# Seven half-size products in the first matmul as well, with part of the sums as accumulating transfers

## The chip, the cores and the metric

One core of one Trainium2 chip. The metric is device time in microseconds (us), the median over the runs of a kernel. The profile's span is shorter than the time (about 1.8 us for the kernel before); the text says which of the two a number is. A run counts as slow when it lies over 1.5% above the fastest run of the same kernel; ratios use fast runs only.

## The reference

```python
m, k, n, p = 1024, 1024, 2048, 1024
h = np.matmul(a, b)                                     # 1024 x 2048
h = 0.5 * h * (1 + np.tanh(np.sqrt(2 / np.pi) * (h + 0.044715 * h ** 3)))
return np.matmul(h, c).astype(np.float32)               # 1024 x 1024
```

## The kernel before

The first product is plain: 16 column tiles of b times two halves of 512 rows of a, 8 matmuls each, in bf16. The second is done with seven products of half-size quarters instead of eight, Winograd's form of Strassen's scheme: it needs sums of quarters of h (s1 to s4) and of c (t1 to t4), and VectorE makes all of them. The sums are fp32r (4 bytes), the plain quarters bf16 (2 bytes) where they are used only as they are.

```python
    # first product: six tiles while b arrives, then the rest
    for k in range(KT):
        ...
        for t in range(N0):
            nc.tensor.matmul(ps[t], bt(k, t), aT[0][:, k, :],
                             start=(k == 0), stop=(k == KT - 1))
    # ... cut ...
    def mm1(t, h):
        p = ppool.tile([128, H], F32, name="ps")
        for k in range(KT):
            nc.tensor.matmul(p, bt(k, t), aT[h][:, k, :],
                             start=(k == 0), stop=(k == KT - 1))
        gelu(t, h, p)
    # ... cut ...
    def sum_s4(i):
        nc.vector.tensor_tensor(pair(s2, i), h12[:, ts(i, 2), :], pair(s2, i), op=SUB)

    def sum_t4(t):
        nc.vector.tensor_tensor(t2[t], t2[t], c21[:, t:t + 1, :], op=SUB)
    # ... cut ...
    for j in R:                                  # s3 x t3, beside it s4 on VectorE
        p = bank()
        prod(p, whole(s3), whole(t3), j)
        nc.vector.tensor_tensor(u3[:, j, :], p, u2[j], op=ADD)
        sum_s4(j)
    for j in R:                                  # s1 x t1 (p5), beside it t4 on VectorE
        p = bank()
        prod(p, whole(s1), pairs(t1), j)
        combine(4 + j, 1, p, u3[:, j, :])
        nc.vector.tensor_tensor(u2[j], p, u2[j], op=ADD)
        sum_t4(2 * j)
        sum_t4(2 * j + 1)
    # ... cut: s4 x c22, h22 x t4, the last tile ...
```

Of the kernel before, what the change touches and what calls it, by code (L numbers as in the profile page):

```python
# [19 lines left out]
def kernel(ctx, tc, a, b, c, out):  # L20
# [22 lines left out]
    b0stage = ctx.enter_context(tc.tile_pool(name="b0stage", bufs=8))  # L43
# [9 lines left out]
    NH = NT // 2  # L53
    aT = [keep.tile([128, KT, H], BF16, name=f"aT{h}", tag=f"A{h}") for h in range(2)]
    WB = W0 + W1
    b_lo = keep.tile([128, KT, WB], BF16, name="b_lo", tag="B0")
    b_hi = keep.tile([128, KT, N - WB], BF16, name="b_hi", tag="B1")

    def bcols(k0, kn, n0, w):
        if n0 < WB:  # L60
            return b_lo[:, k0:k0 + kn, ds(n0, w)]
        return b_hi[:, k0:k0 + kn, ds(n0 - WB, w)]

    def bt(k, t):
        return bcols(k, 1, t * 128, 128)[:, 0, :]


    hq = [[keep.tile([128, NH, H], F32R if h else BF16, name=f"h{h}{g}") for g in range(2)]
          for h in range(2)]
# [19 lines left out]
    for mt in range(4):  # L89
        load_a0(mt, 2 if mt == 3 else 1)  # L90
# [38 lines left out]
    for mt in range(4):  # L129
        if mt < 3:  # L130
            ab.append(cast_a0(mt + 1))
        turn0(mt, ab[mt], (0,) if mt == 3 else (0, 1))
        if mt < 3:
            warm_up(3)
    cast_b0(0)
    for k in range(KT):
        if k + 1 < KT:
            cast_b0(k + 1)
        for t in range(N0):
            nc.tensor.matmul(ps[t], bt(k, t), aT[0][:, k, :],  # L140
                             start=(k == 0), stop=(k == KT - 1))
        if k == 0:
            turn0(3, ab[3], (1,))

    def gelu(t, h, p):
        nc.scalar.activation(hq[h][t // NH][:, t % NH, :], p, AF.Gelu_apprx_tanh)  # L146

    for t in range(N0):
        gelu(t, 0, ps[t])


    def load_b(k0, kn, n0, w):
        nc.gpsimd.dma_start(out=bcols(k0, kn, n0, w), in_=bv[:, k0:k0 + kn, ds(n0, w)])

    ps = [(tpool if t < 2 else ppool).tile([128, H], F32, name="pt" if t < 2 else "ps")
          for t in range(N1)]
    for k in range(0, KT, 4):
        load_b(k, 4, W0, W1)
        for i in range(4):
            for t in range(N1):  # L160
                nc.tensor.matmul(ps[t], bt(k + i, N0 + t), aT[0][:, k + i, :],  # L161
                                 start=(k + i == 0), stop=(k + i == KT - 1))
    for t in range(N1):
        gelu(N0 + t, 0, ps[t])


    def mm1(t, h):
        p = ppool.tile([128, H], F32, name="ps")
        for k in range(KT):
            nc.tensor.matmul(p, bt(k, t), aT[h][:, k, :],  # L170
                             start=(k == 0), stop=(k == KT - 1))
        gelu(t, h, p)

    W2 = 384
    for n0 in range(W0 + W1, N, W2):
        for k in range(0, KT, 4):
            load_b(k, 4, n0, W2)

    a1 = []
    for j in range(4):  # L180
        st = abf.tile([128, K], BF16, name="ab1")
        nc.gpsimd.dma_start(out=st, in_=av[:, 4 + j, :])
        a1.append(st)

    def turn(j):
        ab = a1[j]
        pt = tpool.tile([128, KT, 128], BF16, name="pt")
        for k in range(KT):
            nc.tensor.transpose(pt[:, k, :], ab[:, ts(k, 128)], ident)  # L189
        nc.vector.tensor_copy(aT[1][:, :, ts(j, 128)], pt)  # L190

    for t in range(N0 + N1, NT):
        mm1(t, 0)
        if t == NT - 3:
            turn(0)
        if t == NT - 2:
            turn(1)
            turn(2)
            turn(3)
# [7 lines left out]
    (h11, h12), (h21, h22) = hq  # L207
    c11 = keep.tile([128, NH, H], BF16, name="c11")
    c21 = keep.tile([128, NH, H], BF16, name="c21")
    c22 = keep.tile([128, NH, H], F32R, name="c22")  # L210
    c12 = keep.tile([128, NH, H], BF16, name="c12", tag="A0")
# [5 lines left out]
    load_c(c11, 0, 0)  # L217
    load_c(c22, 1, 1)
    load_c(c21, 1, 0)
    load_c(c12, 0, 1)  # L220

    t1 = [astage.tile([128, 2, H], F32R, name="t1", tag="a_st") for _ in range(4)]
    t2 = [b0stage.tile([128, 1, H], F32R, name="t2", tag="b0_st") for _ in range(8)]
    s1 = keep.tile([128, NH, H], F32R, name="s1")

    def sum_t1(i):
        nc.vector.tensor_tensor(t1[i], c12[:, ts(i, 2), :], c11[:, ts(i, 2), :], op=SUB)  # L227

    def sum_t2(t):
        nc.vector.tensor_tensor(t2[t], c22[:, t:t + 1, :], t1[t // 2][:, t % 2:t % 2 + 1, :], op=SUB)  # L230

    def sum_s1(t):
        nc.vector.tensor_tensor(s1[:, t, :], h21[:, t, :], h22[:, t, :], op=ADD)

    for t in range(NT):
        mm1(t, 1)
        if 3 <= t < 7:
            sum_t1(t - 3)
        if 6 <= t < 10:
            sum_t2(2 * (t - 6))  # L240
            sum_t2(2 * (t - 6) + 1)
        if t == WB // 128:
            t3 = keep.tile([128, NH, H], F32R, name="t3", tag="B0")
        if t >= NH + 1:
            sum_s1(t - NH - 1)
        if WB // 128 <= t < WB // 128 + 4:
            i = t - WB // 128
            nc.vector.tensor_tensor(t3[:, ts(i, 2), :], c22[:, ts(i, 2), :], c12[:, ts(i, 2), :], op=SUB)
    sum_s1(NH - 1)

    s2 = [keep.tile([128, NH // 2, H], F32R, name=f"s2{g}", tag=f"A{g}") for g in range(2)]

# [12 lines left out]
    def sum_t4(t):
        nc.vector.tensor_tensor(t2[t], t2[t], c21[:, t:t + 1, :], op=SUB)

    def bank(w=H):
        return ppool.tile([128, w], F32, name="ps", padded_shape=[128, H])

    def prod(p, lhs, rhs, j, q=slice(0, H)):
        for t in range(NH):
            nc.tensor.matmul(p, lhs(t)[:, ts(j, 128)], rhs(t)[:, q],  # L273
                             start=(t == 0), stop=(t == NH - 1))
# [98 lines left out]
```

## Time and profile before

| | before |
|---|---|
| time, median (3 runs) | 123.95 us |
| span of the profiled run | 122.1 us |
| TensorE busy | 116.1 us (95%) |
| VectorE busy | 64.6 us (53%) |
| first product ends, second begins | 69.0 us |
| second product, up to TensorE's end | 50.2 us |

The page divides the span into 40 slices; a digit is the busy share in tenths. The chain of waits is followed back from the last instruction: what stands in it sets the end, what does not could be longer without harm. For TensorE the starts of successive matmuls give the real pitch, because the listed durations overlap. The prediction shows these lines.

### The profile page before, as it was taken

The numbers are of one execution on the slowest core, as the hardware profiler recorded it, in microseconds if no ns is written. First come the engines' busy times: TensorE is split into PE (matmuls) and PEld (weight loads), VectorE is DVE, ScalarE is ACT, GpSimd is POOL, SyncE is SP. The second block draws the span as 40 slices with busy tenths as digits, with TensorE's granted clock in tenths as the row PEclk, the third lists the DMA queues.
The fourth block names the chain that finished last, engine by engine and source line by source line (L and its number), as shares of the span: only waits on it lengthen the run. The fifth ranks groups of instructions, "written<-read, shape, count | busy, mean of one in ns | idle before, by whom it ended". The sixth has DMA issues, their size and how long they took to land.

```text
span 122.1 us, 1486 instructions
## 1 busy us (share of the span) xinstructions
PE 116.1 (95%) x577; PEld 68.3 (56%) x577; DVE 64.6 (53%) x95; ACT 30.7 (25%) x54; POOL 21.5 (18%) x26
## 2 busy tenths in 40 slices
PE   6977999999998999999999999999999999999990
PEld 2542444444456444444444444468888888888880
DVE  0352340000014200006999999999769999974351
ACT  4454752806331133233323331100000000000000
POOL 2000099132440220000000000797000000000000
PEclk9999999999999999999999999999999999999999
DMA  3999969999999999995000000000600022445425
GB/s 144 351 328 347 413 188 191 198 200 205 209 207 206 329 394 231 206 206 97 0 0 0 5 0 3 3 0 0 258 0 0 5 86 86 157 167 191 163 99 167
DMA packets 12582, 18.44 MB, mean 151 GB/s; under 512 B 800, under 2 KB 7584, under 8 KB 12576
## 3 DMA queue, kind: packets, MB, share of 16 engines
q0 software_dynamic: 7968, 8.91, 39.6%
q1 hardware_dynamic: 4464, 9.37, 20.9%
q10 hardware_dynamic: 144, 0.07, 0.2%
q8 instruction: 4, 0.07, 0.2%
q14 instruction: 2, 0.02, 0.0%
HBM read 20.97 MB, written 4.19 MB: 206 GB/s over the span
## 4 chain that ended last, share of the span: by engine, by line
PE 88%; DMA 6%; SPq 2%; DVE 1%; ACT 0%; issue 0%
PE ps L273 41%; PE ps L170 31%; PE ps L140 8%; DMA b_st<-in_b_dram 6%; PE ps L161 3%; PE pt L161 3%; SPq L78 2%; PE pt L189 1%; DVE aT L190 1%; ACT b_lo L126 0%; SPq L85 0%; DVE ot L342 0%; PE pt L115 0%
## 5 line engine op out<-in xcount | busy, mean ns | idle before, releaser
L146 ACT ACTIVATE h<-ps 128x512 fp32r<-128x512 f32 (+1 forms) x30 | 17.3, 602 | 28.6 <-PE ps L170 26.3
L170 PE MATMUL ps<-aT,b_hi 128*128 128x512 bf16 x96 | 21.4, 379 | 0.0
L170 PE MATMUL ps<-aT,b_lo 128*128 128x512 bf16 x80 | 17.4, 379 | 0.0
L170 PEld LDWEIGHTS <-b_hi 128*128 128x128 bf16 x96 | 9.3, 98 | 10.8
L273 PE MATMUL ps<-t,s 128*128 128x512 f32 x64 | 15.0, 392 | 0.0
L273 PE MATMUL ps<-t,h 128*128 128x512 f32 x64 | 14.8, 389 | 0.0
L273 PE MATMUL ps<-c,h 128*128 128x512 bf16 (+2 forms) x80 | 14.2, 336 | 0.0
L313 POOL COPY lk<-u 128x512 f32<-128x512 f32 x1 | 7.7, 7684 | 33.6 <-ACT u L306 33.6
L273 PEld LDWEIGHTS ps<-t,s 128*128 128x128 f32 x64 | 12.0, 188 | 2.6
L273 PEld LDWEIGHTS ps<-t,h 128*128 128x128 f32 x64 | 12.0, 188 | 2.5
L170 PEld LDWEIGHTS <-b_lo 128*128 128x128 bf16 x80 | 7.8, 98 | 9.4
L227 DVE TENSOR_TENSOR t<-c,c 128x1024 fp32r<-128x1024 bf16 x4 | 4.7, 1222 | 15.8 <-DMA c<-in_c_dram 15.7
L190 DVE COPY aT<-pt 128x1024 bf16<-128x1024 bf16 x4 | 2.7, 689 | 19.4 <-PE pt L189 19.3
L140 PE MATMUL ps<-aT,b_lo 128*128 128x512 bf16 x48 | 10.9, 380 | 0.8 <-DVE b_lo L125 0.8
L273 PEld LDWEIGHTS <-h 128*128 128x128 bf16 x80 | 7.2, 98 | 7.0 <-issue 0.3
L140 PEld LDWEIGHTS <-b_lo 128*128 128x128 bf16 x48 | 4.5, 98 | 6.6 <-DVE b_lo L125 1.1
L215 POOL DMA_DIRECT2D c<-in_c_dram x8 | 5.9, 744 | 11.7 <-PE ps L170 6.0
L296 DVE TENSOR_TENSOR ot<-ps,u 128x512 f32<-128x512 f32 x11 | 7.3, 684 | 1.1 <-PE ps L273 1.1
L101 PE MATMUL ps<-warm 128*128 128x512 bf16 x17 | 6.3, 516 | 1.2 <-DVE warm L49 1.2
L273 PE MATMUL ps<-c,s 128*128 128x512 f32 x32 | 7.4, 389 | 0.0
L273 PEld LDWEIGHTS ps<-c,s 128*128 128x128 f32 x32 | 6.0, 188 | 1.2
L125 DVE CAST b_lo<-b_st 128x384 bf16<-128x384 f32 x8 | 2.9, 368 | 5.1 <-DMA b_st<-in_b_dram 5.1
(40 smaller groups left out, 96.5 us busy)
## 6 DMA issues: line engine op xcount, KB each, us to landing
out_dram<-ot SPq DMA_DIRECT2D x15, 256.0 KB, 2.0
c<-in_c_dram POOLq DMA_DIRECT2D x6, 512.0 KB, 14.8
b_st<-in_b_dram SPq DMA_DIRECT2D x7, 384.0 KB, 8.1
c<-in_c_dram POOLq DMA_DIRECT2D x2, 1024.0 KB, 15.0
a_st<-in_a_dram SPq DMA_DIRECT2D x3, 512.0 KB, 4.1
b_hi<-in_b_dram POOLq DMA_DIRECT2D x4, 384.0 KB, 11.3
b_lo<-in_b_dram POOLq DMA_DIRECT2D x2, 512.0 KB, 7.2
ab<-in_a_dram POOLq DMA_DIRECT2D x4, 256.0 KB, 13.9
```

Of the source, the lines that this page charges most:

```text
L101: nc.tensor.matmul(ps[N0 - 1], warm[:, 0:128], warm, start=True, stop=True)
L125: nc.vector.tensor_copy(b_lo[:, k, 0:HW], b_st[k][:, 0:HW])
L140: nc.tensor.matmul(ps[t], bt(k, t), aT[0][:, k, :], start=(k == 0), stop=(k == KT - 1))
L146: nc.scalar.activation(hq[h][t // NH][:, t % NH, :], p, AF.Gelu_apprx_tanh)
L161: nc.tensor.matmul(ps[t], bt(k + i, N0 + t), aT[0][:, k + i, :], start=(k + i == 0), stop=(k + i == KT - 1))
L170: nc.tensor.matmul(p, bt(k, t), aT[h][:, k, :], start=(k == 0), stop=(k == KT - 1))
L190: nc.vector.tensor_copy(aT[1][:, :, ts(j, 128)], pt)
L215: nc.gpsimd.dma_start(out=dst[:, t:t + 4, :], in_=cv[:, r * NH + t:r * NH + t + 4, ts(q, H)])
L227: nc.vector.tensor_tensor(t1[i], c12[:, ts(i, 2), :], c11[:, ts(i, 2), :], op=SUB)
L273: nc.tensor.matmul(p, lhs(t)[:, ts(j, 128)], rhs(t)[:, q], start=(t == 0), stop=(t == NH - 1))
L296: nc.vector.tensor_tensor(ot, u if swap else p, p if swap else u, op=op)
L313: nc.gpsimd.tensor_copy(last_keep, last)
```

## The change

The intent is to take 16 of the 256 matmuls of the first product away as well. The right half of b (1024 columns) is treated as four quarters; with the four quarters of a it gives h12 and h22 from seven products of 16 matmuls. The left half stays plain. That needs six new sums before these products and two between them. To make room on VectorE, several sums become accumulating transfers: ScalarE or an earlier sum fills the destination, and a transfer issued by GpSimd adds the second operand into it. Three such groups come late: t3, s2 + h12 (s4) and t2 + c21 (t4). The product s1 × t1 (p5) goes second in the last block, and half-width matmuls fill the time between the last turns (transposes) of a. The first stage loads 1024 columns of b instead of 768.

```diff
-    W0 = N0 * 128
+    W0 = N // 2
...
+    for i in range(2):                       # six new sums, two tiles each
+        tt(as1[i], aT[1][:, P2[i], :], aT[1][:, P2[i + 2], :], op=ADD)
+    # ... as2, as3, bt3, b12, bt2 cut ...
+    for j in R:
+        p = bank()
+        prod(p, KH, pairs(bt2), pairs(as2), j)
+        tt(v2[:, j, :], p, v2[:, j, :], op=ADD)
+    for i in range(2):
+        nc.gpsimd.dma_start(out=as2[i], in_=aT[0][:, P2[i + 2], :], accum_op=ADD)
+    for i in range(2):
+        nc.gpsimd.dma_start(out=bt2[i], in_=bx[:, P2[i + 2], :], accum_op=ADD)
+    # ... four more of the seven products cut ...
+    for i in R:                              # t2 = t1 - c22
+        nc.scalar.mul(t2[i], c22[:, P2[i], :], -1.0)
+        nc.gpsimd.dma_start(out=t2[i], in_=t1[:, P2[i], :], accum_op=ADD)
+    c21 = keep.tile([128, NH, H], BF16, name="c21", tag="BX")
+    load_c(c21, 1, 0)
...
     for j in R:
         p = bank()
-        prod(p, whole(h11), whole(c11), j)
-        nc.scalar.activation(u2[j], p, AF.Copy)
+        prod(p, NH, whole(h11), whole(c11), j)
+        nc.scalar.activation(p1[:, j, :], p, AF.Copy)
+    for i in (2, 3, 0, 1):                   # t3 = c22 - c12
+        nc.scalar.mul(t3p(i), c12[:, P2[i], :], -1.0)
+        nc.gpsimd.dma_start(out=t3p(i), in_=c22[:, P2[i], :], accum_op=ADD)
+    # ... p5 = s1 x t1, s3, then u2 = s2 x t2 cut ...
+    for g in range(2):                       # s4 = s2 + h12
+        nc.gpsimd.dma_start(out=s2[g], in_=h12[:, ts(g, KH), :], accum_op=ADD)
+    for i in R:                              # t4 = t2 + c21
+        nc.gpsimd.dma_start(out=t2[i], in_=c21[:, P2[i], :], accum_op=ADD)
+    # ... h12 x c21, s3 x t3, s4 x c22, h22 x t4, the last tile cut ...
```

More of the change, by code (lines that the diff above doesn't have):

```diff
@@ L29 @@
     N0 = 6
-    W0 = N0 * 128
-    N1 = 4
-    W1 = N1 * 128
+    W0 = N // 2
+    KH = KT // 2
+    NH = NT // 2
+    R = range(4)
     av = a.rearrange("(mt p) k -> p mt k", p=128)
@@ L42 @@
     abf = ctx.enter_context(tc.tile_pool(name="abf", bufs=4))
-    b0stage = ctx.enter_context(tc.tile_pool(name="b0stage", bufs=8))
+    b0stage = ctx.enter_context(tc.tile_pool(name="b0stage", bufs=6))
     opool = ctx.enter_context(tc.tile_pool(name="opool", bufs=4))
@@ L51 @@
     make_identity(nc, ident)
-    NH = NT // 2
     aT = [keep.tile([128, KT, H], BF16, name=f"aT{h}", tag=f"A{h}") for h in range(2)]
-    WB = W0 + W1
-    b_lo = keep.tile([128, KT, WB], BF16, name="b_lo", tag="B0")
-    b_hi = keep.tile([128, KT, N - WB], BF16, name="b_hi", tag="B1")
-    def bcols(k0, kn, n0, w):
-        if n0 < WB:
-            return b_lo[:, k0:k0 + kn, ds(n0, w)]
-        return b_hi[:, k0:k0 + kn, ds(n0 - WB, w)]
-    def bt(k, t):
-        return bcols(k, 1, t * 128, 128)[:, 0, :]
-    hq = [[keep.tile([128, NH, H], F32R if h else BF16, name=f"h{h}{g}") for g in range(2)]
-          for h in range(2)]
+    a22 = keep.tile([128, KH, H], F32R, name="a22", tag="A22")
+    b_lo = keep.tile([128, KT, W0], BF16, name="b_lo", tag="B0")
+    bx = keep.tile([128, KT, H], BF16, name="bx", tag="BX")
+    b12 = keep.tile([128, KH, H], F32R, name="b12", tag="BT")
+    b22 = keep.tile([128, KH, H], F32R, name="b22", tag="BR")
+    (h11, h12), (h21, h22) = [[keep.tile([128, NH, H], F32R if h else BF16, name=f"h{h}{g}")
+                               for g in range(2)] for h in range(2)]
     a_st, b_st = {}, {}
@@ L88 @@
     gate = consts.tile([128, 1], F32, name="gate")
-    for mt in range(4):
+    for mt in R:
         load_a0(mt, 2 if mt == 3 else 1)
@@ L128 @@
     ab = [cast_a0(0)]
-    for mt in range(4):
+    for mt in R:
         if mt < 3:
@@ L139 @@
         for t in range(N0):
-            nc.tensor.matmul(ps[t], bt(k, t), aT[0][:, k, :],
+            nc.tensor.matmul(ps[t], b_lo[:, k, ts(t, 128)], aT[0][:, k, :],
                              start=(k == 0), stop=(k == KT - 1))
@@ L143, with gelu, bank @@
             turn0(3, ab[3], (1,))
-    def gelu(t, h, p):
-        nc.scalar.activation(hq[h][t // NH][:, t % NH, :], p, AF.Gelu_apprx_tanh)
+    def gelu(dst, src):
+        nc.scalar.activation(dst, src, AF.Gelu_apprx_tanh)
+    def bank(w=H):
+        return ppool.tile([128, w], F32, name="ps", padded_shape=[128, H])
     for t in range(N0):
-        gelu(t, 0, ps[t])
-    def load_b(k0, kn, n0, w):
-        nc.gpsimd.dma_start(out=bcols(k0, kn, n0, w), in_=bv[:, k0:k0 + kn, ds(n0, w)])
-    ps = [(tpool if t < 2 else ppool).tile([128, H], F32, name="pt" if t < 2 else "ps")
-          for t in range(N1)]
-    for k in range(0, KT, 4):
-        load_b(k, 4, W0, W1)
-        for i in range(4):
-            for t in range(N1):
-                nc.tensor.matmul(ps[t], bt(k + i, N0 + t), aT[0][:, k + i, :],
-                                 start=(k + i == 0), stop=(k + i == KT - 1))
-    for t in range(N1):
-        gelu(N0 + t, 0, ps[t])
-    def mm1(t, h):
-        p = ppool.tile([128, H], F32, name="ps")
-        for k in range(KT):
-            nc.tensor.matmul(p, bt(k, t), aT[h][:, k, :],
-                             start=(k == 0), stop=(k == KT - 1))
-        gelu(t, h, p)
-    W2 = 384
-    for n0 in range(W0 + W1, N, W2):
-        for k in range(0, KT, 4):
-            load_b(k, 4, n0, W2)
+        gelu(h11[:, t, :], ps[t])
     a1 = []
-    for j in range(4):
+    for j in R:
         st = abf.tile([128, K], BF16, name="ab1")
@@ L183 @@
         a1.append(st)
+    nc.gpsimd.dma_start(out=b12, in_=bv[:, 0:KH, W0 + H:N])
+    nc.gpsimd.dma_start(out=b22, in_=bv[:, KH:KT, W0 + H:N])
+    for k in range(0, KT, KH):
+        nc.gpsimd.dma_start(out=bx[:, k:k + KH, :], in_=bv[:, k:k + KH, W0:W0 + H])
     def turn(j):
-        ab = a1[j]
         pt = tpool.tile([128, KT, 128], BF16, name="pt")
         for k in range(KT):
-            nc.tensor.transpose(pt[:, k, :], ab[:, ts(k, 128)], ident)
+            nc.tensor.transpose(pt[:, k, :], a1[j][:, ts(k, 128)], ident)
@@ L190, in turn, with mm1_half @@
         nc.vector.tensor_copy(aT[1][:, :, ts(j, 128)], pt)
-    for t in range(N0 + N1, NT):
-        mm1(t, 0)
-        if t == NT - 3:
-            turn(0)
-        if t == NT - 2:
-            turn(1)
-            turn(2)
-            turn(3)
-    (h11, h12), (h21, h22) = hq
-    c11 = keep.tile([128, NH, H], BF16, name="c11")
-    c21 = keep.tile([128, NH, H], BF16, name="c21")
+        nc.scalar.activation(a22[:, :, ts(j, 128)], aT[1][:, KH:KT, ts(j, 128)], AF.Copy)
+    def mm1_half(t, q):
+        p = bank(256)
+        for k in range(KT):
+            nc.tensor.matmul(p, b_lo[:, k, ts(t, 128)], aT[1][:, k, ts(q, 256)],
+                             start=(k == 0), stop=(k == KT - 1))
+        gelu(h21[:, t, ts(q, 256)], p)
@@ new lines, in mm1, with two @@
+    def mm1(t, h, dst):
+        p = bank()
+        for k in range(KT):
+            nc.tensor.matmul(p, b_lo[:, k, ts(t, 128)], aT[h][:, k, :],
+                             start=(k == 0), stop=(k == KT - 1))
+        gelu(dst, p)
+    mm1(6, 0, h11[:, 6, :])
+    turn(0)
+    mm1(7, 0, h11[:, 7, :])
+    turn(1)
+    turn(2)
+    mm1_half(0, 0)
+    turn(3)
+    mm1_half(1, 0)
+    mm1_half(2, 0)
+    for t in range(3):
+        mm1_half(t, 1)
+    tt = nc.vector.tensor_tensor
+    def two(pool, name, tag):
+        return [pool.tile([128, 2, H], F32R, name=name, tag=tag) for _ in range(2)]
@@ new lines @@
+    as1 = two(astage, "as1", "a_st")
+    as3 = two(astage, "as3", "a_st")
+    bt3 = two(b0stage, "bt3", "b0_st")
+    as2 = two(b0stage, "as2", "b0_st")
+    bt2 = two(b0stage, "bt2", "b0_st")
+    P2 = [slice(2 * i, 2 * i + 2) for i in range(4)]
+    for i in range(2):
+        tt(as1[i], aT[1][:, P2[i], :], aT[1][:, P2[i + 2], :], op=ADD)
+    for i in range(2):
+        tt(as2[i], aT[0][:, P2[i], :], as1[i], op=SUB)
+    for i in range(2):
+        tt(as3[i], aT[0][:, P2[i], :], aT[1][:, P2[i], :], op=SUB)
@@ new lines, with whole, pairs, prod @@
+    for i in range(2):
+        tt(bt3[i], b22[:, P2[i], :], b12[:, P2[i], :], op=SUB)
+    for i in range(2):
+        tt(b12[:, P2[i], :], b12[:, P2[i], :], bx[:, P2[i], :], op=SUB)
+    for i in range(2):
+        tt(bt2[i], b12[:, P2[i], :], b22[:, P2[i], :], op=SUB)
+    for t in range(3, NH):
+        mm1(t, 1, h21[:, t, :])
+    def whole(x, t0=0):
+        return lambda t: x[:, t0 + t, :]
+    def pairs(x):
+        return lambda t: x[t // 2][:, t % 2, :]
+    def prod(p, n, lhs, rhs, j, q=slice(0, H)):
+        for t in range(n):
+            nc.tensor.matmul(p, lhs(t)[:, ts(j, 128)], rhs(t)[:, q],
+                             start=(t == 0), stop=(t == n - 1))
@@ L210, with new_out, add_gelu @@
+    def new_out():
+        return opool.tile([128, H], F32, name="ot")
+    def add_gelu(dst, p, u):
+        ot = new_out()
+        tt(ot, p, u, op=ADD)
+        gelu(dst, ot)
+    c11 = keep.tile([128, NH, H], BF16, name="c11", tag="c11")
+    c12 = keep.tile([128, NH, H], BF16, name="c12")
     c22 = keep.tile([128, NH, H], F32R, name="c22")
-    c12 = keep.tile([128, NH, H], BF16, name="c12", tag="A0")
     def load_c(dst, r, q):
@@ L217 @@
     load_c(c11, 0, 0)
+    load_c(c12, 0, 1)
     load_c(c22, 1, 1)
-    load_c(c21, 1, 0)
-    load_c(c12, 0, 1)
-    t1 = [astage.tile([128, 2, H], F32R, name="t1", tag="a_st") for _ in range(4)]
-    t2 = [b0stage.tile([128, 1, H], F32R, name="t2", tag="b0_st") for _ in range(8)]
-    s1 = keep.tile([128, NH, H], F32R, name="s1")
-    def sum_t1(i):
-        nc.vector.tensor_tensor(t1[i], c12[:, ts(i, 2), :], c11[:, ts(i, 2), :], op=SUB)
-    def sum_t2(t):
-        nc.vector.tensor_tensor(t2[t], c22[:, t:t + 1, :], t1[t // 2][:, t % 2:t % 2 + 1, :], op=SUB)
@@ L232, in sum_s1 @@
-    def sum_s1(t):
-        nc.vector.tensor_tensor(s1[:, t, :], h21[:, t, :], h22[:, t, :], op=ADD)
-    for t in range(NT):
-        mm1(t, 1)
-        if 3 <= t < 7:
-            sum_t1(t - 3)
-        if 6 <= t < 10:
-            sum_t2(2 * (t - 6))
-            sum_t2(2 * (t - 6) + 1)
-        if t == WB // 128:
-            t3 = keep.tile([128, NH, H], F32R, name="t3", tag="B0")
-        if t >= NH + 1:
-            sum_s1(t - NH - 1)
-        if WB // 128 <= t < WB // 128 + 4:
-            i = t - WB // 128
-            nc.vector.tensor_tensor(t3[:, ts(i, 2), :], c22[:, ts(i, 2), :], c12[:, ts(i, 2), :], op=SUB)
@@ L249 @@
-    sum_s1(NH - 1)
-    s2 = [keep.tile([128, NH // 2, H], F32R, name=f"s2{g}", tag=f"A{g}") for g in range(2)]
-    def pair(x, i):
-        return x[i // 2][:, ts(i % 2, 2), :]
-    for i in range(4):
-        nc.vector.tensor_tensor(pair(s2, i), s1[:, ts(i, 2), :], h11[:, ts(i, 2), :], op=SUB)
-    for i in range(4):
-        nc.vector.tensor_tensor(h21[:, ts(i, 2), :], h11[:, ts(i, 2), :], h21[:, ts(i, 2), :], op=SUB)
-    s3 = h21
-    def sum_s4(i):
-        nc.vector.tensor_tensor(pair(s2, i), h12[:, ts(i, 2), :], pair(s2, i), op=SUB)
@@ L265, in sum_t4 @@
-    def sum_t4(t):
-        nc.vector.tensor_tensor(t2[t], t2[t], c21[:, t:t + 1, :], op=SUB)
-    def bank(w=H):
-        return ppool.tile([128, w], F32, name="ps", padded_shape=[128, H])
-    def prod(p, lhs, rhs, j, q=slice(0, H)):
-        for t in range(NH):
-            nc.tensor.matmul(p, lhs(t)[:, ts(j, 128)], rhs(t)[:, q],
-                             start=(t == 0), stop=(t == NH - 1))
-    def whole(x):
-        return lambda t: x[:, t, :]
+    v2 = keep.tile([128, 4, H], F32, name="v2", tag="A1")
@@ new lines, with sum_t1 @@
+    v3 = [abf.tile([128, H], F32, name="v3", tag="ab1") for _ in R]
+    t1 = keep.tile([128, NH, H], F32R, name="t1", tag="B0")
+    def sum_t1(i):
+        tt(t1[:, P2[i], :], c12[:, P2[i], :], c11[:, P2[i], :], op=SUB)
+    for j in R:
+        p = bank()
+        prod(p, KH, whole(bx), whole(aT[0]), j)
+        nc.scalar.activation(v2[:, j, :], p, AF.Copy)
+    for j in R:
+        p = bank()
+        prod(p, KH, whole(bx, KH), whole(aT[0], KH), j)
+        add_gelu(h12[:, j, :], p, v2[:, j, :])
+        if j >= 2:
+            sum_t1(j - 2)
@@ new lines @@
+    for j in R:
+        p = bank()
+        prod(p, KH, pairs(bt2), pairs(as2), j)
+        tt(v2[:, j, :], p, v2[:, j, :], op=ADD)
+        if j >= 2:
+            sum_t1(j)
+    for i in range(2):
+        nc.gpsimd.dma_start(out=as2[i], in_=aT[0][:, P2[i + 2], :], accum_op=ADD)
+    for i in range(2):
+        nc.gpsimd.dma_start(out=bt2[i], in_=bx[:, P2[i + 2], :], accum_op=ADD)
+    for j in R:
+        p = bank()
+        prod(p, KH, pairs(bt3), pairs(as3), j)
+        tt(v3[j], p, v2[:, j, :], op=ADD)
@@ new lines @@
+    for j in R:
+        p = bank()
+        prod(p, KH, whole(b12), pairs(as1), j)
+        add_gelu(h22[:, 4 + j, :], p, v3[j])
+        tt(v2[:, j, :], p, v2[:, j, :], op=ADD)
+    t2 = [astage.tile([128, 2, H], F32R, name="t2", tag="a_st") for _ in R]
+    for i in R:
+        nc.scalar.mul(t2[i], c22[:, P2[i], :], -1.0)
+        nc.gpsimd.dma_start(out=t2[i], in_=t1[:, P2[i], :], accum_op=ADD)
+    c21 = keep.tile([128, NH, H], BF16, name="c21", tag="BX")
+    load_c(c21, 1, 0)
+    for j in R:
+        p = bank()
+        prod(p, KH, whole(b22), pairs(as2), j)
+        add_gelu(h12[:, 4 + j, :], p, v2[:, j, :])
@@ new lines, with sum_s1 @@
+    s1 = {}
+    def sum_s1(i):
+        s1[i] = b0stage.tile([128, 2, H], F32R, name="s1", tag="b0_st")
+        tt(s1[i], h21[:, P2[i], :], h22[:, P2[i], :], op=ADD)
+    sum_s1(2)
+    sum_s1(3)
+    for j in R:
+        p = bank()
+        prod(p, KH, pairs(bt2), whole(a22), j)
+        add_gelu(h22[:, j, :], p, v3[j])
+    sum_s1(0)
+    sum_s1(1)
+    s2 = [keep.tile([128, KH, H], F32R, name=f"s2{g}", tag=tag) for g, tag in ((0, "A0"), (1, "BR"))]
+    for i in (2, 3, 0, 1):
+        tt(s2[i // 2][:, P2[i % 2], :], h11[:, P2[i], :], s1[i], op=SUB)
@@ L279, in halves, with t3p, t3t @@
+    t3 = two(b0stage, "t3", "b0_st") + [keep.tile([128, KH, H], F32R, name="t3b", tag="BT")]
+    def t3p(i):
+        return t3[i] if i < 2 else t3[2][:, P2[i - 2], :]
+    def t3t(t):
+        return t3[t // 2][:, t % 2, :] if t < 4 else t3[2][:, t - 4, :]
     def halves(x):
         return lambda t: x[t // 4][:, t % 4, :]
-    def pairs(x):
-        return lambda t: x[t // 2][:, t % 2, :]
-    def ones(x):
-        return lambda t: x[t][:, 0, :]
-    def new_out():
-        return opool.tile([128, H], F32, name="ot")
@@ L291, in store, with combine @@
     def store(ot, m, q0, w=H, queue=nc.sync):
         queue.dma_start(out=out[ts(m, 128), ds(q0, w)], in_=ot[:, 0:w])
-    def combine(m, q, p, u, op=ADD, swap=False):
+    def combine(m, q, p, u):
         ot = new_out()
-        nc.vector.tensor_tensor(ot, u if swap else p, p if swap else u, op=op)
+        tt(ot, p, u, op=ADD)
         store(ot, m, q * H)
-    R = range(4)
-    u2 = [abf.tile([128, H], F32, name="u2", tag="ab1") for _ in R]
-    u3 = keep.tile([128, 4, H], F32, name="u3", tag="B1")
+    p1 = keep.tile([128, 4, H], F32, name="p1", tag="A22")
@@ L303 @@
+    p5 = keep.tile([128, 4, H], F32, name="p5", tag="A1")
+    u2 = keep.tile([128, 4, H], F32, name="u2", tag="c11")
+    u3 = [abf.tile([128, H], F32, name="u3", tag="ab1") for _ in R]
     for j in R:
         p = bank()
-        prod(p, whole(h11), whole(c11), j)
-        nc.scalar.activation(u2[j], p, AF.Copy)
+        prod(p, NH, whole(h11), whole(c11), j)
+        nc.scalar.activation(p1[:, j, :], p, AF.Copy)
+    for i in (2, 3, 0, 1):
+        nc.scalar.mul(t3p(i), c12[:, P2[i], :], -1.0)
+        nc.gpsimd.dma_start(out=t3p(i), in_=c22[:, P2[i], :], accum_op=ADD)
@@ new lines @@
+    for j in R:
+        p = bank()
+        prod(p, NH, pairs(s1), whole(t1), j)
+        nc.scalar.activation(p5[:, j, :], p, AF.Copy)
+    for i in R:
+        tt(h21[:, P2[i], :], h11[:, P2[i], :], h21[:, P2[i], :], op=SUB)
+    s3 = h21
+    for j in R:
+        p = bank()
+        prod(p, NH, halves(s2), pairs(t2), j)
+        tt(u2[:, j, :], p, p1[:, j, :], op=ADD)
+        tt(p5[:, j, :], u2[:, j, :], p5[:, j, :], op=ADD)
+    for g in range(2):
+        nc.gpsimd.dma_start(out=s2[g], in_=h12[:, ts(g, KH), :], accum_op=ADD)
@@ L307 @@
+    for i in R:
+        nc.gpsimd.dma_start(out=t2[i], in_=c21[:, P2[i], :], accum_op=ADD)
     for j in range(3):
         p = bank()
-        prod(p, whole(h12), whole(c21), j)
-        combine(j, 0, p, u2[j])
-    last = u2[3]
-    last_keep = opool.tile([128, H], F32, name="lk", bufs=1)
-    nc.gpsimd.tensor_copy(last_keep, last)
+        prod(p, NH, whole(h12), whole(c21), j)
+        combine(j, 0, p, p1[:, j, :])
     for j in R:
         p = bank()
-        prod(p, halves(s2), ones(t2), j)
-        nc.vector.tensor_tensor(u2[j], p, u2[j], op=ADD)
+        prod(p, NH, whole(s3), t3t, j)
+        tt(u3[j], p, u2[:, j, :], op=ADD)
+        combine(4 + j, 1, p, p5[:, j, :])
@@ L318 @@
     for j in R:
         p = bank()
-        prod(p, whole(s3), whole(t3), j)
-        nc.vector.tensor_tensor(u3[:, j, :], p, u2[j], op=ADD)
-        sum_s4(j)
+        prod(p, NH, halves(s2), whole(c22), j)
+        combine(j, 1, p, p5[:, j, :])
     for j in R:
         p = bank()
-        prod(p, whole(s1), pairs(t1), j)
-        combine(4 + j, 1, p, u3[:, j, :])
-        nc.vector.tensor_tensor(u2[j], p, u2[j], op=ADD)
-        sum_t4(2 * j)
-        sum_t4(2 * j + 1)
-    for j in R:
-        p = bank()
-        prod(p, halves(s2), whole(c22), j)
-        combine(j, 1, p, u2[j])
@@ L334 @@
-    for j in R:
-        p = bank()
-        prod(p, whole(h22), ones(t2), j)
-        combine(4 + j, 0, p, u3[:, j, :], op=SUB, swap=True)
+        prod(p, NH, whole(h22), pairs(t2), j)
+        combine(4 + j, 0, p, u3[j])
     for q0, w, queue in ((0, 256, nc.sync), (256, 128, nc.scalar), (384, 128, nc.sync)):
         p = bank(w)
-        prod(p, whole(h12), whole(c21), 3, q=ds(q0, w))
+        prod(p, NH, whole(h12), whole(c21), 3, q=ds(q0, w))
         ot = new_out()
-        nc.vector.tensor_tensor(ot[:, 0:w], p, last_keep[:, ds(q0, w)], op=ADD)
+        tt(ot[:, 0:w], p, p1[:, 3, ds(q0, w)], op=ADD)
```

## The prediction

> **What bounds the kernel now.** I read the page first (busy tenths by slice, granted clock), then the chain of waits that ended last, then the groups of instructions by shape, then timelines of single stretches.
>
> The page, busy tenths and clock in 40 slices of about 3.05 us:
>
> ```profile
> PE   6977999999998999999999999999999999999990
> ...
> DVE  0352340000014200006999999999769999974351
> ...
> PEclk9999999999999999999999999999999999999999
> DMA  3999969999999999995000000000600022445425
> ```
>
> TensorE is full from the fifth slice on at full clock. VectorE is idle between the casts and about 56 us, and the DMA engines rest after about 58 us: there is spare capacity for the sums that the change adds. The chain of waits in order of time (start us, us, what):
>
> ```profile
> 11.57 0.82 PE ps L140 x3
> 12.39 0.22 PE pt L115 x4
> 12.62 9.23 PE ps L140 x42
> ...
> 35.66 0.45 PE pt L189 x8
> 36.11 1.73 PE ps L170 x8
> 37.83 0.46 PE pt L189 x8
> 38.30 0.02 issue
> 38.32 0.70 DVE aT L190
> 39.02 0.04 issue
> 39.06 0.61 PE pt L189 x8
> 39.67 29.35 PE ps L170 x136
> 69.02 50.17 PE ps L273 x240
> ```
>
> From 11.57 to 119.2 us there is only TensorE work, except 0.7 us between transposes. So the kernel gains what it saves in TensorE time and nothing else, and only if no new wait appears. Real pitches, since the listed durations overlap: 29.35 us over 136 matmuls is 215.8 ns for a bf16 matmul of 512 columns. For fp32r I take the starts of like groups in the TensorE timeline:
>
> ```profile
> 80.76 7.63 PE L273 MATMUL ps<-t,s 128*128 128x512 f32 x32
> 88.23 7.42 PE L273 MATMUL ps<-t,h 128*128 128x512 f32 x32
> 95.48 7.42 PE L273 MATMUL ps<-t,s 128*128 128x512 f32 x32
> ```
>
> 95.48 − 88.23 = 7.25 us over 32 is 226.6 ns. The first fp32r group, which follows bf16, takes 7.47 us: a switch costs about 0.2 us. Matmuls of 256 columns (in the tail) start 109.2 ns apart.
>
> **What the Trainium skill says.** "TensorE: Matmul & The Clock Gate", section "Wait — 56ns, not 53.3ns?", gives N ÷ 2.4 GHz + about 2.5 ns warm, 215.7 ns for 512 columns: the trace agrees (215.8). It does not give fp32r; I use 226.6. "VectorE: DVE Perf Modes", the section on the TRN2 errata, gives (N+151)/0.96 ns for an fp32 tensor_tensor: 691 and 1224 ns for 512 and 1024; the trace has 684 and 1218, but successive ones start only 0.60 and 1.14 us apart, and that is what a chain costs. "DMA: Bandwidth & Descriptors", section "Queues, rings and completion order", says each engine round-robins between queues packet by packet, so a second queue takes bandwidth from the first; in this trace the overlap (17 to 18 us) is too short to tell. "Collectives: The Full Stack", "Why ReduceScatter is half of AllGather", says an accumulating transfer reads two sources and the reads limit it. No run here has such a transfer yet; it is the largest unknown.
>
> **The change, part by part.**
>
> 1. Matmuls. The first product has 2 × 16 × 8 = 256 matmuls of 215.8 ns, 55.24 us. After: the left half of b stays plain: 64 for the upper rows, 40 for the lower rows in full width, 48 of half width. The right half becomes seven products of 4 × 4 = 16: two in bf16 (32), five in fp32r (80). So 136 × 0.2158 + 48 × 0.1092 + 80 × 0.2266 = 29.35 + 5.24 + 18.13 = 52.72 us. Saved: **2.5 us**. Sixteen matmuls fewer are worth 3.45, but fp32r takes 0.86 back. The second product has the same seven products in the same types; only the order changes.
>
> 2. Type switches. Before there is one bf16-to-fp32r switch; after there are three. **+0.4 us**.
>
> 3. Turns of a. Before, 35.66 to 39.67 holds 1.73 us of matmuls, so the turns cost 2.28. After: four of 0.45 plus the rest of one VectorE copy (0.69 less the 0.46 of the next turn), since half-width matmuls need only turns 0 and 1. About 2.1: **−0.2 us**.
>
> 4. First stage. It loads 1024 columns of b instead of 768 before anything else. The pace now is set by the arrivals:
>
> ```profile
> 16.07 0.52 ACT L126 ACTIVATE b_lo<-b_st 128x384 bf16<-128x384 f32 x1 [0.43 <-DMA b_st<-in_b_dram]
> 17.04 0.52 ACT L126 ACTIVATE b_lo<-b_st 128x384 bf16<-128x384 f32 x1 [0.44 <-DMA b_st<-in_b_dram]
> 18.01 0.52 ACT L126 ACTIVATE b_lo<-b_st 128x384 bf16<-128x384 f32 x1 [0.45 <-DMA b_st<-in_b_dram]
> ```
>
> 393 KB every 0.97 us, 405 KB/us. A 524 KB row block then takes 1.29 us, against 6 × 0.2158 = 1.295 us of matmuls per block: the stage turns from TensorE-bound to evenly balanced. Block 1 arrives at 12.19 + 2 × 0.32 = 12.83, its VectorE cast takes 0.43 (the 128x512 cast of a takes 427 ns), TensorE starts it at 13.3 and ends block 7 at 13.3 + 7 × 1.295 = 22.4, against 21.85 now: +0.5. The loads of the lower a, released by block 4, may overlap the last blocks; I add 0.25. **+0.75 us**.
>
> 5. Sums on VectorE. Twelve of 128x1024 in 12 × 1.14 = 13.7 us, from about 30 us on, done near 44; first needed near 49 (third of the seven products). Then 28 reads of PSUM at 0.60 and four sums for t1: 21 us within the 25 us of the seven products. With six banks I find no stop, the tightest being near the fifth product, where VectorE needs 1.2 us per bank and TensorE 0.91. The s1 sums end near 73; p5, put second in the last block, needs them near 74.5. The 7.7 us copy on GpSimd disappears, but nothing waited for its end.
>
> 6. Accumulating transfers: as2 and bt2 (four of 512 KB destination), t2 and t3 (eight), s2 (two of 1 MB), t2 again (four). Each needs its destination's old reader to finish, and has a deadline. Estimate: 4 bytes of destination plus 2 of bf16 source read per element at the 405 KB/us above, 1.9 us per 512 KB, after 1.6 us of start and as much to the landing. as2 and bt2: released near 53, landing near 58, 60, 62, 64; wanted at 60.0, 60.5, 63.7, 64.1. That is even. s2 and the second t2: released near 89, together 6.3 MB of reads, plus eleven output stores of 262 KB in the same stretch, 2.9 MB: 22 us, while the last t2 is wanted near 110, 21 us later. Even again. I allow **+0.4 us** on average for both, with a long tail upwards.
>
> Sum: −2.5 + 0.4 − 0.2 + 0.75 + 0.4 = −1.15 us, so 123.95 − 1.15 = **122.8 us**, 0.9% less. The 1.85 us between the span (122.1) and the time stay.
>
> **The rivals.** (a) The accumulating transfers miss their deadlines. For it: two deadlines are even by my estimate, and they stand in one issuing queue, in order. At half the estimated rate as2 would land 3 to 4 us late, bt2 another 4 and s2 some 5: 130 us or more. Against: the order of the groups seems laid out around these deadlines, and one stop late in the block gives the next transfers time. (b) VectorE becomes the bound. For it: the page shows it at 9 tenths through the second product already. Against: the moved sums lie where it is idle now, and the t4, t3 and s4 sums leave it. If it held banks back, +1 to +2 us, 124 to 125. (c) The first stage becomes DMA-bound throughout, b and a contending: up to +2 instead of +0.75, 124. (d) All is hidden and the first stage loses nothing: −2.5 + 0.4 − 0.2 = −2.3, 121.65 us, which is 1.9%: so even the best case I can build does not quite pass 2%.
>
> **Range and chances.** The best case puts the lower end near 121.7; the tail of (a) sets the upper end at 125.2. Faster by over 2% (under 121.5) needs a saving that I do not see: 0.08. Slower by over 2% (above 126.4) needs (a) at a clearly lower rate than estimated: 0.13. The rest, 0.79, within 2%.
>
> **What would show it.** Right: 480 − 16 matmul equivalents, fp32r starts near 226 ns apart in the first product; the six-tile stage ending near 22.4 to 22.9; the right-half products beginning near 42, the last block near 67, and 50 us of TensorE from there as now, plus 0.2. VectorE sums done before the third product asks. Wrong: TensorE waiting on a DMA of as2, bt2, s2 or t2 (rival a); on VectorE with banks full (b); on b_st in the last blocks (c). A span shorter than 119.8 us would mean that TensorE time was cut somewhere that I count as unchanged.

## The result

| | before | after |
|---|---|---|
| time, median (4 runs each) | 123.96 us | 128.91 us (128.03 to 130.26) |
| span of the profiled run | 122.1 us | 126.3 us |
| first matmul of the second product starts | 68.9 us | 66.6 us |
| bytes moved by the core's DMA | 18.4 MB | 30.5 MB |

One of the four runs after (130.26) counts as slow; the median of the other three is 128.28 us. The ratio of the fast runs is 1.037 (95% interval 1.029 to 1.046): slower by 3.7%. A ratio here is the mean time of one kernel's fast runs over that of the other's in the same rounds, so not quite the ratio of the medians. The predicted 122.8 us was wrong, and so was its range (121.7 to 125.2). The first product is 2.3 us shorter (68.86 against 66.55), as the change wanted. The second product lost that and more.

The page of the changed kernel, the same rows as before:

```profile
PE   6985999989999999999999999999977999984990
...
DVE  0343231248999639999999999867541354233551
...
PEclk9999999999999999999999999999998599999999
DMA  3999999999999999199519999999999999995734
```

TensorE now has two dents late in the span (7, 7 and 8, 4), and the granted clock falls to half in one slice. The DMA row is full from slice 21 on, where it was almost empty before: these are the accumulating transfers. The chain of waits, late part (start us, us, what):

```profile
41.62 32.02 PE ps L233 x144
...
75.51 0.90 POOL t3b L352
...
87.56 0.84 POOL s L366
...
90.64 24.76 DMA t<-c
115.40 0.04 issue
115.45 7.98 PE ps L233 x50
```

The chain leaves TensorE at 73.6 us and comes back only at 115.45. Between lies one transfer of the last group of t2 that took 24.8 us from its issue to its landing, and before it the issues that stood in its way on GpSimd. TensorE's timeline shows the two stops:

```profile
88.00 5.35 PE L233 MATMUL ps<-c,h 128*128 128x512 bf16 x24
93.00 0.81 PE L233 MATMUL ps<-t,h 128*128 128x512 f32 x2
95.63 0.73 PE L233 MATMUL ps<-t,h 128*128 128x512 f32 x2 [1.82 <-DMA t<-c]
...
104.18 7.44 PE L233 MATMUL ps<-c,s 128*128 128x512 f32 x32
111.46 1.07 PE L233 MATMUL ps<-t,h 128*128 128x512 f32 x4
112.82 0.73 PE L233 MATMUL ps<-t,h 128*128 128x512 f32 x2 [0.29 <-DMA t<-c]
115.45 6.18 PE L233 MATMUL ps<-t,h 128*128 128x512 f32 x26 [1.90 <-DMA t<-c]
121.47 1.94 PE L233 MATMUL ps<-c,h 128*128 128x256 bf16 x24
```

The group s3 × t3 starts at 93.00 and the next at 104.18: 11.18 us, where the same group takes 7.46 without a wait (100.55 − 93.09 in e1, below). So 3.7 us are lost to the wait for t3. About 2.0 of them are the stop itself. The other 1.7 come after it: from 97.1 to 100.5 us the granted clock was half and matmuls started 427 ns apart. It isn't shown that the time would be 1.7 us shorter without this: the fast run of 128.28 us was at full clock throughout and was no faster than the profiled one (128.03). In e3 a run at full clock reaches the next product earlier and waits there for s4. The group h22 × t4 takes 121.47 − 111.46 = 10.0 us instead of 7.25, lost to the wait for t4: 2.8 us. Together 6.5 us. Taken from 126.3 they leave 119.8 us.

The DMA queues in five stretches of the changed kernel (us, then length and busy time of each engine, clock, DMA share, GB/s; an accumulating transfer's bytes are counted once, as written):

```profile
54.00:61.00 7.00, 7.00 (x33) 5.79 (x32) 7.00 (x12) 1.27 (x2) 1.61 (x2) 1.00 1.06 257
66.00:76.00 10.00, 10.00 (x48) 5.54 (x47) 10.00 (x12) 8.96 (x16) 4.02 (x6) 1.00 1.05 188
85.00:92.00 7.00, 7.00 (x33) 4.15 (x33) 4.75 (x8) 0.00 (x0) 4.39 (x6) 1.00 1.06 210
94.00:101.00 7.00, 5.37 (x16) 4.29 (x17) 1.64 (x4) 0.00 (x0) 0.00 (x0) 0.76 1.06 296
102.00:111.00 9.00, 9.00 (x41) 7.36 (x40) 3.21 (x6) 0.00 (x0) 0.00 (x0) 1.00 1.07 299
```

In all five the DMA engines are busy throughout (share just over 1.00). By the packets in the trace the queue held as2 and bt2 from 53 to 62 us, t2 from 65.5 to 77, the load of c21 from 77 to 83, t3 from 83 to 93, s4 from 93 to 102 and t4 from 102 to 115, the last two beside output stores. From 104 to 112 us the trace has about 49 packets per us of each of the two, of 4 KB for t4 and of 2 KB for the stores; that agrees with the turns by packet which the prediction could not yet tell from the trace before. From 65.5 us until the last t4 landed at 115.4 the queue never ran empty. Groups with a bf16 source wrote about 257 GB/s (as2, bt2), those with an fp32r source about 188 (t2 from t1) and 210 (t3 from c22); why these two differ was not tested.

### The profile page after: what moved, and what is told of

Read it like the earlier page. It is cut to its first block, busy times and chain, and to the rows that moved or that the text cites. A ratio compares the mean times of both kernels' runs of the same rounds, so it can differ in the third digit from the quotient of the medians.

```text
span 126.3 us, 1585 instructions
## 1 busy us (share of the span) xinstructions
PE 115.8 (92%) x585; PEld 76.5 (61%) x585; DVE 77.6 (61%) x107; ACT 46.1 (36%) x77; POOL 28.2 (22%) x41
## 4 chain that ended last, share of the span: by engine, by line
PE 54%; DMA 26%; issue 8%; POOL 5%; SPq 2%; DVE 1%; ACT 1%; POOLq 0%
PE ps L233 32%; DMA t<-c 20%; PE ps L174 10%; PE ps L132 7%; DMA b_st<-in_b_dram 6%; PE ps L167 4%; SPq L70 2%; POOL t3b L352 1%; POOL s L366 1%; POOL t L352 1%; PE pt L160 1%; POOL t L368 1%; ACT t3b L351 1%; SPq L77 1%; DVE aT L161 1%
## 5 line engine op out<-in xcount | busy, mean ns | idle before, releaser
L233 PE MATMUL ps<-t,s 128*128 128x512 f32 x64 | 14.9, 392 | 0.0
L338 DVE TENSOR_TENSOR ot<-ps,p 128x512 f32<-128x512 f32 x11 | 7.5, 689 | 11.4 <-DMA out_dram<-ot 9.1
L233 PE MATMUL ps<-c,h 128*128 128x512 bf16 (+2 forms) x80 | 14.4, 337 | 0.0
L138 ACT ACTIVATE h<-ot 128x512 bf16<-128x512 f32 (+1 forms) x16 | 9.3, 624 | 12.5 <-DVE ot L241 12.5
L174 PE MATMUL ps<-aT,b_lo 128*128 128x512 bf16 x56 | 12.6, 379 | 0.0
L241 DVE TENSOR_TENSOR ot<-ps,v 128x512 f32<-128x512 f32 x16 | 10.5, 689 | 3.2 <-PE ps L233 3.2
L138 ACT ACTIVATE h<-ps 128x512 bf16<-128x512 f32 (+2 forms) x19 | 9.4, 536 | 8.3 <-PE ps L174 6.2
L132 PE MATMUL ps<-aT,b_lo 128*128 128x512 bf16 x48 | 10.7, 379 | 1.5 <-DVE b_lo L117 1.5
L117 DVE CAST b_lo<-b_st 128x512 bf16<-128x512 f32 x8 | 3.4, 426 | 7.0 <-DMA b_st<-in_b_dram 7.0
L233 PE MATMUL ps<-as,bt 128*128 128x512 f32 x32 | 7.7, 396 | 0.0
L233 PE MATMUL ps<-as,b 128*128 128x512 f32 x32 | 7.4, 389 | 0.0
L233 PE MATMUL ps<-aT,bx 128*128 128x512 bf16 x32 | 7.1, 379 | 0.0
L118 ACT ACTIVATE b_lo<-b_st 128x512 bf16<-128x512 f32 x8 | 5.0, 630 | 5.4 <-DMA b_st<-in_b_dram 5.3
## 6 DMA issues: line engine op xcount, KB each, us to landing
t<-c POOLq DMA_DIRECT2D x6, 512.0 KB, 19.6
s<-h POOLq DMA_DIRECT2D x2, 1024.0 KB, 14.4
```

Source lines behind the costliest of these rows:

```text
L117: nc.vector.tensor_copy(b_lo[:, k, 0:HW], b_st[k][:, 0:HW])
L118: nc.scalar.activation(b_lo[:, k, HW:W0], b_st[k][:, HW:W0], AF.Copy)
L132: nc.tensor.matmul(ps[t], b_lo[:, k, ts(t, 128)], aT[0][:, k, :], start=(k == 0), stop=(k == KT - 1))
L138: nc.scalar.activation(dst, src, AF.Gelu_apprx_tanh)
L174: nc.tensor.matmul(p, b_lo[:, k, ts(t, 128)], aT[h][:, k, :], start=(k == 0), stop=(k == KT - 1))
L233: nc.tensor.matmul(p, lhs(t)[:, ts(j, 128)], rhs(t)[:, q], start=(t == 0), stop=(t == n - 1))
```

## The experiments

Theory Q: an accumulating transfer reads its source and its destination, so it fills the DMA engines; one after another, the late groups pass their deadlines. Rivals: V, VectorE could not hold these sums anyway; L, such a transfer simply takes long from issue to landing; F, the time went into the first product. "The corrected kernel" below is the kernel of the first experiment.

### e1: the three late groups back on VectorE

```diff
-    for i in (2, 3, 0, 1):
-        nc.scalar.mul(t3p(i), c12[:, P2[i], :], -1.0)
-        nc.gpsimd.dma_start(out=t3p(i), in_=c22[:, P2[i], :], accum_op=ADD)
+        tt(t3p(j), c22[:, P2[j], :], c12[:, P2[j], :], op=SUB)   # beside s2 x t2
-    for g in range(2):
-        nc.gpsimd.dma_start(out=s2[g], in_=h12[:, ts(g, KH), :], accum_op=ADD)
-    for i in R:
-        nc.gpsimd.dma_start(out=t2[i], in_=c21[:, P2[i], :], accum_op=ADD)
+        sum_s4(j)       # beside h12 x c21; the last one beside s3 x t3
+        sum_t4(j - 1)   # beside s3 x t3
```

> The three late accumulating sums (t3, s2 + h12, t2 + c21) go back to VectorE. Theory Q (the accumulating transfers read source and destination, so they fill the DMA engines back to back from 65 to 115 us and two of them come late): no stop of TensorE on a DMA is left, 3.9 + 2.8 us vanish from the 126.3 us span, so span 119.4 to 120.0 and time 121.2 to 121.9, about 2% below the kernel before. Theory V (the sums were moved because VectorE cannot hold them): VectorE keeps PSUM banks back and the time is 123 us or more. Theory F (the first product's fp32r products or the longer first stage cost the time): stays at 126 us or more.

Measured: correct, 122.34 us (122.05 to 122.67), ratio to the kernel before 0.987 (0.985 to 0.990), span of the profiled run 119.8. Its chain of waits, end:

```profile
67.07 21.40 PE ps L233 x95
...
88.53 28.49 PE ps L233 x142
```

TensorE runs through from 67 us to the end. The span is the one computed above from the changed kernel without its stops. VectorE is busy 75% of the span and holds nothing up, so V falls. The first product is as in the changed kernel (the second starts at 66.6 us in both), so F falls too. The profiled span is as expected, but the median time is 0.4 us above the upper end, mostly because it exceeds the span by 2.2 us in this kernel's runs instead of 1.85; why is not known. This version beats both kernels: 1.3% under the one before.

### e2: only t3 on VectorE

The first part of e1's edit alone.

> Only t3 on VectorE. Theory Q: the stop before the s3 x t3 products (3.9 us) vanishes and the queue is 10 us of transfers shorter, so s2 starts near 90 instead of 93.5 us; the last t2 still comes some 2 us late: span near 121.5, time 122.5 to 124.5. Theory L (an accumulating transfer simply takes long from issue to landing, 12 to 20 us, whatever else is queued): the last t2 keeps its 20 us or more from issue to landing and the second stop grows to some 6 us, because TensorE arrives 4 us earlier: time 127 us or more.

Measured: correct, 123.42 us (123.10 to 123.73), ratio 0.996 (0.993 to 0.999), span 121.9. The issues of the s4 transfers and TensorE's only stop on a DMA:

```profile
s<-h POOLq DMA_DIRECT2D x2, 1024.0 KB, 8.3
```

```profile
108.73 1.52 PE L233 MATMUL ps<-t,h 128*128 128x512 f32 x6
110.63 6.21 PE L233 MATMUL ps<-t,h 128*128 128x512 f32 x26 [0.38 <-DMA t<-c]
```

The same two s4 transfers land in a median 8.3 us after issue, against 14.4 in the changed kernel, because t3 is no longer ahead of them. The last t4 stop shrinks to about 0.5 us although TensorE comes there earlier. (The profiled span is 2.1 us longer than in e1: 0.7 of it arises in this product and 0.9 already in the first stage, where tile 6 starts at 22.86 instead of 21.93.) That is Q and speaks against L: the time to landing is time in the queue.

### e3: only t4 on VectorE

The last part of e1's edit alone.

> Only the last t2 sum (t2 + c21) on VectorE. Theories Q and L alike: the second stop (2.8 us) vanishes, the first (3.9 us) stays: span near 123.5, time 125.2 to 126.8. The output stores land in 2 to 3 us again towards the end. If the time is at 128 or more, the second stop was not the transfer's.

Measured: correct, 127.13 us (126.00 to 128.10; one run slow), ratio 1.023 (1.017 to 1.029).

```profile
95.55 0.73 PE L233 MATMUL ps<-t,h 128*128 128x512 f32 x2 [1.39 <-DMA t<-c]
...
105.25 6.64 PE L233 MATMUL ps<-c,s 128*128 128x512 f32 x28 [1.68 <-DMA s<-h]
```

The stop on t3 stays and the stop on t4 is gone, as expected. I had not expected the new one: in this run no half clock followed the first stop, so TensorE reached s4 × c22 earlier, at 102.5 us, and caught the s4 transfer still under way. The median of all four runs lies 0.3 us above the range that I gave; that of the three fast ones, 126.70, lies within it.

### e4: plain copies in place of the additions (wrong result)

```diff
-        nc.gpsimd.dma_start(out=t3p(i), in_=c22[:, P2[i], :], accum_op=ADD)
+        nc.gpsimd.dma_start(out=t3p(i), in_=c22[:, P2[i], :])
```

and the same for s2 and the last t2.

> Wrong result on purpose: the same late transfers at the same places in the queue, with the same bytes written, but as plain converting copies without the addition. Theory Q (the second read is what costs): 512 KB of destination takes some 1.3 us instead of 2.0 to 2.6, the queue catches up, both stops vanish or shrink under 1 us: time 121.2 to 122.5. Theory L (issue, order in the queue or latency is what costs, not the addition): both stops stay, time 127 to 130.

Measured: wrong as intended, 121.97 us (121.85 to 122.42), ratio 0.986 (0.982 to 0.989). The stretches of t3, then of s4:

```profile
85.00:88.00 3.00, 3.00 (x15) 2.50 (x14) 2.47 (x4) 0.00 (x0) 0.14 (x1) 1.00 1.14 418
90.00:95.00 5.00, 5.00 (x24) 2.90 (x23) 2.07 (x3) 0.00 (x0) 1.39 (x3) 1.00 1.12 415
```

The same destinations at the same places in the queue are written at 415 to 418 GB/s instead of 210 (t3), and no stop is left. So it is the addition that costs, not issue, order or latency. L falls here as well.

### e5: t3 with a bf16 source

```diff
-        nc.scalar.mul(t3p(i), c12[:, P2[i], :], -1.0)
-        nc.gpsimd.dma_start(out=t3p(i), in_=c22[:, P2[i], :], accum_op=ADD)
+        nc.scalar.mul(t3p(i), c22[:, P2[i], :], -1.0)
+        nc.gpsimd.dma_start(out=t3p(i), in_=c12[:, P2[i], :], accum_op=ADD)
...
-        tt(h21[:, P2[i], :], h11[:, P2[i], :], h21[:, P2[i], :], op=SUB)
+        tt(h21[:, P2[i], :], h21[:, P2[i], :], h11[:, P2[i], :], op=SUB)
```

Both factors of s3 × t3 change sign, so the result stays.

> The changed kernel with one type changed: the t3 transfers add the bf16 quarter c12 onto a negated copy of c22 (so t3 has the other sign, and s3 too), where it added the fp32r quarter c22 onto a negated c12. Theory R (the bytes read, source plus destination, set the time): 6 instead of 8 bytes read per element, so the four t3 transfers move some 260 KB of destination per us instead of 208, 8 us instead of 10.2; the stop before s3 x t3 shrinks from 3.9 to some 1.5 to 2.2 us and the last t2 lands 2 us earlier; time 126.3 to 128.0 in the fast runs, 1.5 to 2.5 us under the changed kernel. Theory W (the written fp32 bytes or the descriptors set it): the rate stays near 208 and the time near 128 to 130.

Measured: correct, 125.79 us (125.56 to 126.17), ratio 1.016 (1.013 to 1.018).

```profile
85.00:91.00 6.00, 5.95 (x28) 3.57 (x28) 4.15 (x6) 0.00 (x0) 3.66 (x6) 1.00 1.09 279
```

```profile
112.08 7.65 PE L233 MATMUL ps<-t,h 128*128 128x512 f32 x26 [1.87 <-DMA t<-c]
```

t3 is written at 279 GB/s instead of 210. Per element written, 4 + 2 bytes are read instead of 4 + 4: 279 × 6 / 4 = 419 and 210 × 8 / 4 = 420 GB/s of reads. So the bytes read set the time of these additions (theory R). A plain copy is another case: that of s4 in e4 reads 2 bytes for each 4 written and was still written at 415. The gain is somewhat larger than I had expected, about 2.7 us by the ratios of fast runs instead of 1.5 to 2.5. The stop on t3 vanishes altogether, but TensorE still idles 0.4 us for s4 and 0.3 and 1.9 us for t4, and around the last stop the clock is half from 111.8 to 115.2 us.

### e6: s4 and t4 as accumulating transfers on the kernel before

```diff
+    for g in range(2):
+        nc.gpsimd.dma_start(out=s2[g], in_=h12[:, ts(g, 4), :], accum_op=ADD)
+    for t in range(NH):
+        nc.gpsimd.dma_start(out=t2[t], in_=c21[:, t:t + 1, :], accum_op=ADD)
-        sum_s4(j)
-        sum_t4(2 * j)
-        sum_t4(2 * j + 1)
```

with the signs of s2 and t2 turned so that both are additions.

> The kernel before with the sums s4 (h12) and t4 (c21) as accumulating transfers, all else as it was. Theory Q: its queue is empty from 58 us, s2 is released near 88 and wanted near 103, t2 is wanted from 110 to 111.5: 2.1 MB at 250 and 2.1 MB at 200 KB/us fit, with a stop of 0 to 1 us at the end; time 123.8 to 125.0. Theory L (an accumulating transfer needs 12 to 20 us whatever is queued) or a cost of the transfers to TensorE itself: stops before s4 and t4, time 126 or more.

Measured: correct, 124.12 us (123.94 to 124.55), ratio 1.002 (1.000 to 1.005). No stop on a DMA; the two s4 transfers landed in a median 7.9 us. With nothing ahead of it in the queue the same kind of transfer costs no measurable time here (at most 0.5%), and it neither slows TensorE down nor gains anything, because VectorE was not the bound.

### e7: half-width matmuls undone, on the corrected kernel

```diff
-    mm1_half(0, 0)
     turn(3)
-    mm1_half(1, 0)
-    mm1_half(2, 0)
-    for t in range(3):
-        mm1_half(t, 1)
...
-    for t in range(3, NH):
+    for t in range(NH):
```

> On the corrected kernel (late sums on VectorE, 122.3 us): the half-width matmuls between the last turns of a undone, full-width ones after the fourth turn instead. TensorE then waits for a transpose buffer and for the last copy to land: about 0.2 and 0.75 us instead of the 0.75 in all now: time 0.2 to 0.7 us longer, 122.5 to 123.0. If it is the same or shorter, the half-width matmuls cost in their own pitch what they save in waiting.

Measured: correct, 123.35 us (6 runs, 123.13 to 123.61), ratio to before 0.995 (0.993 to 0.998). That is 1.0 us over the corrected kernel, more than the 0.2 to 0.7 expected. The stop before the first full-width matmul:

```profile
29.25 13.99 PE L174 MATMUL ps<-aT,b_lo 128*128 128x512 bf16 x62 [0.79 <-DVE aT L161]
```

From tile 6 to the first of the seven products it takes 43.07 − 22.56 = 20.5 us, against 41.56 − 21.93 = 19.6 in e1. The half-width part is worth its place. The two kernels ran in different rounds, each against the kernel before; the traces show 0.9 of the 1.0 us.

### e8: p5 third, on the corrected kernel

The two groups exchanged: s2 × t2 before s1 × t1.

> On the corrected kernel (122.3 us): product s2 x t2 second and p5 (s1 x t1) third in the last block, the other way round. The s2 sums end on VectorE near 77 us, TensorE would ask for them near 73.4: a stop of TensorE of about 3 us that nothing gives back: time 124.8 to 125.8. If the stop is shorter than 1 us, the order was not needed.

Measured: correct, 126.95 us (125.40 to 127.09), ratio 1.022 (1.017 to 1.027).

```profile
76.72 16.53 PE L233 MATMUL ps<-t,s 128*128 128x512 f32 x64 [2.40 <-DVE s L321]
```

The stop of 2.4 us on the s2 sums is as expected. The group behind it takes 16.5 us, where it took 14.9 in e1, since the clock was half from 76.7 to 80.1 us: 1.7 us on top, which I had left out. So the median lies above the range; the one run whose clock hardly fell (0.998) took 125.40 us and lies within it. The order is needed.

## Why the prediction was wrong

- **Step 1 (matmuls, −2.5 us)** held. The seven products take 66.55 − 41.46 = 25.09 us in the changed kernel; 32 × 0.2158 + 80 × 0.2266 is 25.03. The first product is 2.3 us shorter.
- **Step 2 (switches, +0.2 us each)** was misread. In the kernel before, the first fp32r group takes 0.2 us longer because its first matmul is listed only 28 ns after the last bf16 one. The bf16 group ahead of it is shorter by as much, 80.76 − 68.86 = 11.90 us where 56 × 0.2158 is 12.08:

```profile
68.86 12.25 PE L273 MATMUL ps<-c,h 128*128 128x512 bf16 x56
```

Both groups together leave about 0.03 us for a switch, and the 25.09 us above, with one switch in them, leave 0.06.

- **Step 3 (turns, −0.2 us)** saved nothing: the turns cost 2.28 us in both kernels. But e7 shows that they would have cost 0.9 more without the half-width matmuls.
- **Step 4 (first stage, +0.75 us)** was too high. Tile 6 starts at 21.8 us, 0.15 later than its counterpart before. The second block of b arrived at 12.24 us instead of the 12.83 worked out, and then one every 1.27 us. Why the first loads were faster than scaled, I did not test.
- **Step 5 (VectorE)** held. The s1 sums ended at 72.5 us (73 foreseen), and e1 shows VectorE carrying the three late groups besides.
- **Step 6 (accumulating transfers, +0.4 us) is the step that failed.** It measured about +6.5 us in the profiled run. The mechanism, rival (a), was right, and so was the rate for a bf16 source: 1.9 us for 512 KB worked out, 524 KB at 257 GB/s is 2.0. The deadlines of as2 and bt2, which the prediction called even, were met: they landed from 56.2 to 62.3 us, about 2 us before the times worked out. Two things were left out. First, t2 and t3 have fp32r sources: 8 bytes read per element, not 6, so 2.5 to 2.8 us each (e5). Second, and more: I let s4 and t4 start in an empty queue near 89 us and gave t3 no deadline. The queue was full from 65.5 us with t2 (11.5 us), c21 (5.5) and t3 (10). So t3 came 2 us late, s4 began at 93 instead of 89 and t4 ended at 115 instead of 111. Summed in order, with the missing groups, the prediction's own read rate leads there: t2 and t3 read 4.2 MB each, c21 2.1, s4 and t4 3.15 each, the stores 2.9: 19.7 MB at 405 GB/s are 48.6 us, from 65.5 to 114.
- **What can follow a stop** was not in the prediction at all. In the profiled run of the changed kernel 1.7 of the 6.5 us are lost while the clock is half after the first stop. It does not follow every stop: 1.9 us of idle time before 115.45 brought none.
- **The best case** of the prediction, 121.65 us, was close: e1 and e4, without stops, measured 122.34 and 121.97. In part that was luck: it counts about 0.3 us too much for the two switches, takes off 0.2 us for turns that were not saved, and leaves out the 0.15 of the first stage.

## What to carry to other kernels

An accumulating transfer takes a sum from VectorE, but it costs the DMA engines the bytes of source and destination in reads; add up the whole queue in its order, loads and stores included, against the time at which each tile is wanted, before moving sums there. Here VectorE had time to spare for the late sums (busy 75% in e1, with no stop of TensorE on it); moving them back kept the gain of the change. And an order that avoids a stop of TensorE can be worth more than the stop: from the start of the second product to the last group e8's profiled run takes 4.4 us longer than e1's, with 2.4 us of listed idle time.

## What the Trainium skill lacked or had wrong

- "DMA: Bandwidth & Descriptors" says that only GpSimd's queue can accumulate (the table in "SWDGE vs HWDGE vs iDMA") but gives no rate for it. Between SBUF tiles the runs show 257 to 279 GB/s written with a bf16 source and 188 to 210 with an fp32r source into fp32r, and 415 to 418 as a plain copy. This agrees with the two-reads argument of the collectives page that the prediction cites, which is made there for the add of a ReduceScatter: 376 to 420 GB/s of reads in every addition.
- "TensorE: Matmul & The Clock Gate", in the table of "Why this matters for your kernels", warns of idle gaps over about 3 us. Idle times of 1.8 us (before 95.63 us in the changed kernel), 1.9 us (e5) and 2.4 us (e8) already came with 3.4 us at half clock; others of 1.4 and 1.7 us (e3) and 1.9 us (before 115.45 us in the changed kernel) did not. No page gives the pitch of fp32r matmuls (226.6 ns for 512 columns here).
- No page has the size of the effect of accumulating transfers on stores beside them: 256 KB output stores landed in a median 5.5 us in the changed kernel, 2.0 before, and 9.1 us of VectorE's idle time there went to waiting for them, without reaching TensorE.
